# Down projection of a hybrid encoder: six of eleven pairs of K blocks as seven block products

## The chip, the cores and the metric

The kernel runs on one core of one Trainium2 chip. The metric is the device time of one execution in microseconds. TensorE (PE) multiplies, VectorE (DVE), ScalarE (ACT) and GpSimd (POOL) work elementwise, and SyncE (SP) issues most of the DMA transfers. Before the change the median of three runs is 1108.37 us (1108.06 to 1108.92).

## What is computed

Two layers of an encoder on 256 tokens of width 1024, everything in float32: a half-step SwiGLU block, a mixing block with two attention branches, and a second half-step SwiGLU block. The change lies in the SwiGLU blocks, which run four times in all.

```python
D_MODEL = 1024; SEQ = 256; DEPTH = 2; D_FF = 2816

def swiglu(x, w_gate, w_up, w_down):
    return (jax.nn.silu(x @ w_gate) * (x @ w_up)) @ w_down

for l in range(DEPTH):
    x = x + 0.5 * swiglu(rms_norm(x, ffn1_norm[l]), ffn1_w_gate[l], ffn1_w_up[l], ffn1_w_down[l])
    ...
    x = x + merged @ w_out[l]
    x = x + 0.5 * swiglu(rms_norm(x, ffn2_norm[l]), ffn2_w_gate[l], ffn2_w_up[l], ffn2_w_down[l])
```

## The kernel before

**Products.** Tokens stand in two tiles of 128 (t = 0, 1). A float32 number is carried as a high part in the fast matmul format (F32R) and the rest as a low part. `three` (L161) therefore emits three matmuls for each product of a 128x128 block of activations and a 128x512 block of weights: high by high, high by low, low by high.

**Weights.** `load` (L127) fetches 512 KB into one of four raw buffers (`raw`), copies it on ACT into the high part `wh` (L133) and subtracts on DVE to get the low part `wl` (L134). `wh` and `wl` have six buffers each (RING), and one comes back when the last matmul that reads it is done. SP issues the transfers in program order and waits for a free raw buffer at each.

**An FFN.** `ffn` (L294) has a gate/up phase and a down phase. Gate/up runs over eleven chunks c of 256 hidden columns: four loads of two K blocks each, then for each t 24 matmuls (eight K blocks by three) into a bank of `ps_g`, then Silu on ACT (`sg`, L323) and a multiplication on DVE (`hh`, L325). The transposes of `hh` (`turn`, L300) are deferred by H_LAG = 7.9 matmul groups; they write a bank of `ps_tp`, which `split_to` divides into `hi` and `lo` (L176, L177).

The down phase, `out_rows` (L278), runs over 22 rows of K blocks, 128 rows of the weights each. A row's 1024 columns are two halves d of 512. It adds into four PSUM banks acc[t][d], one row at a time (12 matmuls) up to row 17, and the last four rows bank by bank; when a bank is complete, x gets half of it on DVE (L292), and the norm of the next stage is deferred by NORM_LAG = 4 groups. The norm's transposes (L193) read the new x, and what follows them on DVE and ACT (`xg`, `xh`, `xl`) feeds the next stage.

**Order.** PE's order is the order of the program. The orders of DVE, ACT and SP are set by a scheduler when the program is built, each engine then takes its instructions strictly in that order.

Of the kernel before, what the change touches and what calls it, by code (L numbers as in the profile page):

```python
# [48 lines left out]
HEAD = 128  # L49


@with_exitstack
def hybrid_encoder(ctx, tc, x, w_gu1, w_d1, w_in, b_gate, qk_gain, rpb, sink, t5,
# [73 lines left out]
    def load(src, nk, n, tag="raw"):  # L127
        raw = ring.tile([P, 2, 512], F32, name="raw", tag="raw", bufs=RAW)
        wh = ring.tile([P, 2, 512], F32R, name="wh", tag="wh", bufs=RING)
        wl = ring.tile([P, 2, 512], F32R, name="wl", tag="wl", bufs=RING)  # L130
        r, h, lo = (w[:, :nk, :n] for w in (raw, wh, wl))
        nc.sync.dma_start(r, src)
        linked("act", lambda: nc.scalar.activation(h, r, AF.Copy))  # L133
        linked("dve", lambda: nc.vector.tensor_tensor(lo, r, h.bitcast(F32), ALU.subtract))  # L134
        return wh, wl
# [140 lines left out]
    def out_rows(get, nk, w, l, groups, scale, after):  # L276
        acc = [[ps_acc.tile([P, 512], F32, name="acc", tag=tag, bufs=n) for tag, n in pair] for pair in ACC]
        k0 = 0  # L278
        for g in (*[1] * (nk - sum(groups)), *groups):
            pieces = [(k, *rows(w, l, k)) for k in range(k0, k0 + g)]  # L280
            k0 += g
            order = [(d, p) for d in range(2) for p in pieces]
            if k0 < nk:
                order.sort(key=lambda e: e[1][0])
            for t in range(T):
                for d, (k, wh, wl) in order:
                    xh, xl = get(t, k)
                    three(acc[t][d], xh, xl, wh[:, d, :], wl[:, d, :], k == 0, k == nk - 1)
                    tick(1)
                    if k == nk - 1:  # L290
                        xd = xs[t][:, d * 512:(d + 1) * 512]
                        nc.vector.scalar_tensor_tensor(xd, acc[t][d], scale, xd, op0=ALU.mult, op1=ALU.add)  # L292
                        after(t, d)

    def ffn(l, n, w_gu, w_d, after):
        with tc.tile_pool(name="ffn", bufs=1) as fp:
            hs = {}
            tps = {}

            def turn(c, t, hh):  # L300
                if t == 0:
                    tps[c] = ps_tp.tile([P, 2, 2, P], F32, name="tp", tag="tp")
                tp = tps[c]
                for i in range(2):
                    nc.tensor.transpose(tp[:, i, t, :], hh[:, i * P:(i + 1) * P], ident)  # L305
                if t == T - 1:
                    hi = fp.tile([P, 2, 2, P], F32R, name="hi", tag="hi", bufs=NFC)
# [386 lines left out]
```

## Time and profile before

| | us |
|---|---|
| median of three runs | 1108.37 |
| the profiled execution | 1108.37 |
| its span, first to last instruction | 1106.5 |
| first down projection, first matmul to its end | 136.6 to 198.1 |
| DVE waiting for the high part of weights (L134 for L133) | 182.7 in 179 waits |
| ACT waiting for PE in the down projections and w_out (L133 for L164) | 125.2 in 83 waits |

A row of the timeline is: start, duration, engine, line, operation, what it writes and reads, its shape, the count of merged instructions, and in square brackets how long the engine was idle before it and for whom. In a row of groups the duration is the mean of one in nanoseconds. A row of windows gives, for a stretch of the span, the busy time of each engine with its count of instructions, then the granted TensorE clock, the share of the transfers' engines and GB/s. Matmuls overlap in the pipeline, so their distance is read from start to start and not from their duration. A row of transfers gives the median time from issue to landing.

### The profile page before, as it was taken

How to read it: one execution, taken by the hardware profiler on the slowest of the kernel's cores; microseconds unless marked ns; L12 is line 12 of the kernel's file. 1: busy time of each engine (PE TensorE's matmuls, PEld its weight loads, DVE VectorE, ACT ScalarE, POOL GpSimd, SP SyncE). 2: the span in 40 equal slices, each digit the busy share in tenths (PEclk: the TensorE clock that was granted, in tenths of full speed). 3: DMA queues.
4: the chain of work that ended last, by engine and by line, in shares of the span. 5: the costliest groups of instructions: out<-in, count | busy, mean ns of one | idle time of the engine just before them, and what ended most of it. 6: DMA issues, size and time to landing. Idle time of an engine off the chain costs nothing.

```text
span 1106.5 us, 14361 instructions
## 1 busy us (share of the span) xinstructions
PE 1096.3 (99%) x5223; PEld 906.1 (82%) x5223; DVE 700.5 (63%) x987; ACT 600.4 (54%) x914; POOL 103.9 (9%) x101
## 2 busy tenths in 40 slices
PE   9999999999999999999999999999999999999998
PEld 7788888888888888888888888888888888888887
DVE  6655644888887655564475565457888767555542
ACT  6544543788764554454364544347877546454431
POOL 1000000143420000000000000003434000000000
PEclk9999999999999999999999999999999999999999
DMA  7665565765655556556656556647565555646561
GB/s 238 227 188 192 175 212 165 214 189 150 192 183 154 186 175 193 187 176 213 181 156 209 168 187 208 194 119 240 183 190 184 166 171 163 209 161 195 203 192 57
DMA packets 95399, 203.23 MB, mean 184 GB/s; under 512 B 7200, under 2 KB 13376, under 8 KB 95328
## 3 DMA queue, kind: packets, MB, share of 16 engines
q1 hardware_dynamic: 95104, 202.17, 57.7%
q8 instruction: 41, 0.67, 0.3%
q0 software_dynamic: 224, 0.14, 0.1%
q14 instruction: 30, 0.25, 0.1%
HBM read 201.22 MB, written 1.06 MB: 183 GB/s over the span
## 4 chain that ended last, share of the span: by engine, by line
PE 90%; DVE 4%; ACT 3%; issue 2%; DMA 1%; ACTq 0%; DVEq 0%
PE g L162 19%; PE g L164 19%; PE g L163 18%; PE acc L164 9%; PE acc L162 9%; PE acc L163 9%; PE tp L305 2%; DVE wl L134 2%; ACT wh L133 1%; PE tp L193 1%; PE pt L451 1%; PE sc L430 1%; PE g L229 1%; PE po L465 1%; PE br L163 1%
## 5 line engine op out<-in xcount | busy, mean ns | idle before, releaser
L134 DVE TENSOR_TENSOR wl<-raw,wh 128x1024 fp32r<-128x1024 f32 (+1 forms) x368 | 447.0, 1219 | 196.5 <-ACT wh L133 182.7
L133 ACT ACTIVATE wh<-raw 128x1024 fp32r<-128x1024 f32 (+1 forms) x368 | 383.6, 1049 | 209.9 <-PE acc L164 125.2
L162 PE MATMUL g<-wh,xh 128*128 128x512 f32 (+1 forms) x976 | 390.2, 400 | 0.0
L164 PE MATMUL g<-wh,xl 128*128 128x512 f32 (+1 forms) x976 | 379.4, 389 | 0.0
L163 PE MATMUL g<-wl,xh 128*128 128x512 f32 (+1 forms) x976 | 377.8, 387 | 0.4 <-DVE wl L134 0.4
L164 PEld LDWEIGHTS g<-wh,xl 128*128 128x128 f32 x976 | 183.4, 188 | 40.5 <-DVE xl L177 1.3
L163 PEld LDWEIGHTS g<-wl,xh 128*128 128x128 f32 x976 | 184.2, 189 | 31.9 <-DVE wl L134 0.8
L162 PEld LDWEIGHTS g<-wh,xh 128*128 128x128 f32 x976 | 183.7, 188 | 31.5 <-issue 0.9
L323 ACT ACTIVATE sg<-g,rs_y 128x256 f32<-128x256 f32 x88 | 41.7, 474 | 181.6 <-PE g L164 181.4
L162 PE MATMUL acc<-wh,hi 128*128 128x512 f32 x352 | 138.5, 394 | 0.0
L164 PE MATMUL acc<-wh,lo 128*128 128x512 f32 x352 | 137.3, 390 | 0.0
L163 PE MATMUL acc<-wl,hi 128*128 128x512 f32 x352 | 137.1, 389 | 0.0
L325 DVE SCALAR_TENSOR_TENSOR hh<-g,rs_y,sg 128x256 f32<-128x256 f32 x88 | 42.3, 481 | 139.4 <-ACT sg L323 139.4
L164 PEld LDWEIGHTS acc<-wh,lo 128*128 128x128 f32 x352 | 66.1, 188 | 13.9
L163 PEld LDWEIGHTS acc<-wl,hi 128*128 128x128 f32 x352 | 66.2, 188 | 13.4
L162 PEld LDWEIGHTS acc<-wh,hi 128*128 128x128 f32 x352 | 66.1, 188 | 13.3
L168 POOL TENSOR_TENSOR rs_y<-ms,mhalf 128x1 f32<-128x1 f32 x12 | 7.2, 600 | 654.6 <-DVE ms L214 647.4
L443 POOL TENSOR_TENSOR S<-S,sm 128x512 f32<-128x512 f32 x32 | 37.1, 1159 | 71.7 <-DVE sm L442 45.3
L436 ACT ACTIVATE S<-S,mx 128x256 f32<-128x256 f32 x64 | 31.8, 498 | 7.5 <-DVE mx L433 7.4
L305 PEld LDWEIGHTS tp<-ident,hh 128*128 128x128 f32 x176 | 24.6, 140 | 11.3
L292 DVE SCALAR_TENSOR_TENSOR x<-acc,x 128x512 f32<-128x512 f32 x24 | 16.6, 690 | 26.6 <-PE acc L164 26.6
L305 PE MATMUL tp<-ident,hh 128*128 128x128 f32 x176 | 33.3, 271 | 0.0
(133 smaller groups left out, 925.8 us busy)
## 6 DMA issues: line engine op xcount, KB each, us to landing
raw<-in_w_gu SPq DMA_DIRECT2D x176, 512.0 KB, 4.6
raw<-in_w_d SPq DMA_DIRECT2D x88, 512.0 KB, 3.7
raw<-in_w_in SPq DMA_DIRECT2D x64, 512.0 KB, 4.5
raw<-in_w_out SPq DMA_DIRECT2D x16, 512.0 KB, 3.5
bb<-in_b_gate SPq DMA_DIRECT2D x16, 256.0 KB, 3.5
raw<-in_w_bsw SPq DMA_DIRECT2D x8, 512.0 KB, 4.1
raw<-in_w_bna SPq DMA_DIRECT2D x8, 512.0 KB, 3.5
t5b<-vec_d SPq DMA_DIRECT2D x16, 192.0 KB, 3.5
```

The lines of the kernel that those rows point to most:

```text
L133: linked("act", lambda: nc.scalar.activation(h, r, AF.Copy))
L134: linked("dve", lambda: nc.vector.tensor_tensor(lo, r, h.bitcast(F32), ALU.subtract))
L162: nc.tensor.matmul(ps, xh, wh, start=first, stop=False)
L163: nc.tensor.matmul(ps, xh, wl, start=False, stop=False)
L164: nc.tensor.matmul(ps, xl, wh, start=False, stop=last)
L193: nc.tensor.transpose(tp[:, i, :], xs[t][:, k * P:(k + 1) * P], ident)
L292: nc.vector.scalar_tensor_tensor(xd, acc[t][d], scale, xd, op0=ALU.mult, op1=ALU.add)
L305: nc.tensor.transpose(tp[:, i, t, :], hh[:, i * P:(i + 1) * P], ident)
L323: nc.scalar.activation(sg, ps[:, :FC], AF.Silu, scale=rstd[t])
L325: nc.vector.scalar_tensor_tensor(hh, ps[:, FC:], rstd[t], sg, op0=ALU.mult, op1=ALU.mult)
L436: nc.scalar.activation(S_[:, t, :], S_[:, t, :], AF.Exp, bias=mx[:, t:t + 1], scale=-1.0, accum_out=sm[:, t:t + 1])
L443: nc.gpsimd.tensor_tensor(S_, S_, sm.unsqueeze(2).to_broadcast([P, T, S]), ALU.mult)
```

## The change

A pair c is two rows of K blocks (2c and 2c+1), so that the pair's share of the down projection is a product of a 2x2 block matrix of activations (two token tiles by two K blocks) and a 2x2 block matrix of weights (two K blocks by two column halves). For six of the eleven pairs it is now computed as seven block products, in the form with 15 additions known as Strassen's in Winograd's variant. `PLAN` names the kind of each pair: S is the old way, F and G are seven products.

- Activations: for an F or G pair, `turn` copies the four transposed blocks to SBUF on ACT, makes four sums of them on DVE, and splits seven blocks instead of four.
- Weights: `differences` makes four differences of 128x512 blocks on DVE (`u`, `v`), which are then split. For G pairs this is done in the down phase. For F pairs (1 and 3) `prepare` does it beside gate/up, at chunks 2 and 5, into buffers of their own, and the rows are fetched again in the down phase for the blocks used as they are.
- The corner block (product 1) is split into two buffers of 128x512 with tag `xg`, one high and one low.
- Products 2, 3 and 4 add into the banks acc[0][0], acc[0][1], acc[1][0]; products 1, 6, 5, 7 into four extra banks, of `ps_g` and `ps_tp`, over all six pairs.
- After pair 8, `combine` adds the four extra sums into x on DVE (one copy on ACT); pairs 9 and 10 run behind it bank by bank as the last four rows did.
- `out_rows` now takes a range of rows; in S pairs two rows are done bank by bank. Its other user, w_out, is called twice with four rows.

The diff, cut:

```diff
+PLAN = "SFGFGSGSGSS"
+PREP = {2: 1, 5: 3}
+NS = sum(kind != "S" for kind in PLAN)
...
+    def parts(r, nk=2, n=512):
         wh = ring.tile([P, 2, 512], F32R, name="wh", tag="wh", bufs=RING)
         wl = ring.tile([P, 2, 512], F32R, name="wl", tag="wl", bufs=RING)
+        split_to(wh[:, :nk, :n], wl[:, :nk, :n], r)
+        return wh, wl
...
+            SLOT = ((1, 2), (0, 3))
...
             def turn(c, t, hh):
...
-                    split_to(hi, lo, tp)
-                    hs[c] = (hi, lo)
+                m = 4 if PLAN[c] == "S" else 7
+                hi = fp.tile([P, m, P], F32R, name=f"hi{m}", tag=f"hi{m}", bufs=NS if m == 7 else NFC - NS)
+                lo = fp.tile([P, m, P], F32R, name=f"lo{m}", tag=f"lo{m}", bufs=NS if m == 7 else NFC - NS)
+                if m == 7:
+                    a = fp.tile([P, 8, P], F32, name="a", tag="sums", bufs=3)
+                    nc.scalar.activation(a[:, :4, :], tp, AF.Copy)
+                    for to, x, y, op in ((4, 0, 3, ALU.add), (6, 1, 0, ALU.subtract), (5, 4, 1, ALU.subtract),
+                                         (7, 2, 5, ALU.subtract)):
+                        nc.vector.tensor_tensor(a[:, to, :], a[:, x, :], a[:, y, :], op)
+                    split_to(hi, lo, a[:, 1:, :])
+                else:
+                    split_to(hi, lo, tp)
+                hs[c] = (hi, lo)
...
+            def differences(r0, r1, into):
+                sub = lambda to, x, y: nc.vector.tensor_tensor(to, x, y, ALU.subtract)
+                u = fp.tile([P, 2, 512], F32, name="u", tag="sums", bufs=3)
+                sub(u[:, 0, :], r1[:, 1, :], r0[:, 1, :])
+                sub(u[:, 1, :], r0[:, 1, :], r0[:, 0, :])
+                us = into("u", u)
+                v = fp.tile([P, 2, 512], F32, name="v", tag="sums", bufs=3)
+                sub(v[:, 0, :], r1[:, 1, :], u[:, 1, :])
+                sub(v[:, 1, :], r1[:, 0, :], v[:, 0, :])
+                return us, into("v", v)
+
+            def prepare(c):
+                def into(name, r):
+                    hl = [fp.tile([P, 2, 512], F32R, name=f"{name}{p}{c}", tag=f"{name}{p}{c}") for p in "hl"]
+                    split_to(*hl, r)
+                    return hl
+                stored[c] = differences(block_row(2 * c), block_row(2 * c + 1), into)
+
+            def sevens(c):
+                r0 = block_row(2 * c, n=1 if c in stored else 2)
+                r1 = block_row(2 * c + 1)
+                corner = [act.tile([P, 512], F32R, name=f"c{p}", tag="xg", bufs=2) for p in "hl"]
+                split_to(*corner, r0[:, 0, :])
+                low = parts(r1)
+                us, vs = stored.get(c) or differences(r0, r1, lambda name, r: parts(r))
+                half = lambda pair, i: [p[:, i, :] for p in pair]
+                return (("1", 0, corner), ("2", 1, half(low, 0)), ("3", 6, half(low, 1)), ("5", 3, half(us, 1)),
+                        ("6", 4, half(vs, 0)), ("4", 2, half(vs, 1)), ("7", 5, half(us, 0)))
...
+                    for name, slot, (wh, wl) in sevens(c):
...
+                        three(bank, *[h[:, slot, :] for h in hs[c]], wh, wl, first, final and name in extra)
+                        tick(1)
+                    if final:
+                        combine(extra)
...
+                nc.scalar.activation(p1[:, 0, :], acc["1"], AF.Copy, scale=0.5)
...
+                u2 = plus(p1[:, 1, :], "6", p1[:, 0, :])
+                u3 = plus(p16[:, 0, :], "7", u2)
+                u4 = plus(p16[:, 1, :], "5", u2)
+                u5 = plus(ends[:, 0, :], "5", u3)
+                plus(xs[0][:, :512], "1", xs[0][:, :512])
+                for (t, d), u in (((0, 1), u4), ((1, 0), u3), ((1, 1), u5)):
+                    xd = xs[t][:, d * 512:(d + 1) * 512]
+                    nc.vector.tensor_tensor(xd, xd, u, ALU.add)
...
             for c in range(NFC):
...
+                if c in PREP:
+                    prepare(PREP[c])
```

The change moves work on DVE at three places that matter later. Numbers at the ends of names tell the buffers' generations apart.

First place: DVE in the first down projection. Before, it had one split for each row of weights and one low part of activations, here from the seventh row's on (wl_1318):

```order
L134 TENSOR_TENSOR wl_1318<-raw_1316,wh_1317 128x1024
L134 TENSOR_TENSOR wl_1336<-raw_1334,wh_1335 128x1024
L177 TENSOR_TENSOR lo_1241<-tp_1191,hi_1240 128x512
L134 TENSOR_TENSOR wl_1354<-raw_1352,wh_1353 128x1024
L134 TENSOR_TENSOR wl_1372<-raw_1370,wh_1371 128x1024
```

Now, at the same place (wl_1409 is the low part of pair 3's second row, cl_1358 the corner of pair 2, u_1445, v_1452, wl_1442 and wl_1449 belong to pair 4, cl_1405 is the corner of pair 3):

```order
L182 TENSOR_TENSOR wl_1409<-raw_1402,wh_1408 128x1024
L182 TENSOR_TENSOR lo4_1313<-tp_1263,hi4_1312 128x512
L182 TENSOR_TENSOR cl_1358<-raw_1353,ch_1357 128x512
L342 TENSOR_TENSOR u_1445<-raw_1435,raw_1433 128x512
L342 TENSOR_TENSOR v_1452<-raw_1435,u_1445 128x512
L182 TENSOR_TENSOR wl_1442<-raw_1435,wh_1441 128x1024
L342 TENSOR_TENSOR v_1452<-raw_1435,v_1452 128x512
L182 TENSOR_TENSOR wl_1449<-u_1445,wh_1448 128x1024
L182 TENSOR_TENSOR cl_1405<-raw_1400,ch_1404 128x512
```

Work for pair 4 now stands ahead of pair 3's corner, and its first row here waits for the transfer into raw_1435, which by SP's order goes into the buffer that raw_1402 leaves.

Second place: DVE at the end of the first down projection. Before, four updates of x stood there, each behind its bank, and between them the norm of the next stage. Now, from the last row of pair 10 (wl_1679) to the first update (wl_1796 and wl_1802 are weights of the next stage, p1, p16 and ends the combination's sums):

```order
L182 TENSOR_TENSOR wl_1679<-raw_1676,wh_1678 128x1024
L406 SCALAR_TENSOR_TENSOR p1_1646<-g_1342,p1_1646 128x512
L182 TENSOR_TENSOR wl_1796<-raw_1793,wh_1795 128x1024
L406 SCALAR_TENSOR_TENSOR p16_1647<-tp_1349,p1_1646 128x512
L406 SCALAR_TENSOR_TENSOR p16_1647<-tp_1338,p1_1646 128x512
L182 TENSOR_TENSOR wl_1802<-raw_1799,wh_1801 128x1024
L406 SCALAR_TENSOR_TENSOR ends_1648<-tp_1338,p16_1647 128x512
L416 TENSOR_TENSOR x1_83<-x1_83,p16_1647 128x512
L298 SCALAR_TENSOR_TENSOR x0_82<-acc_1282,x0_82 128x512
```

The update x0_82<-acc_1282, which PE's next transposes read, now stands behind eight operations that follow the last weights.

Third place: DVE at chunk 5 of the first FFN's gate/up. Before, the stretch of the same chunks read:

```order
L134 TENSOR_TENSOR wl_660<-raw_658,wh_659 128x1024
L325 SCALAR_TENSOR_TENSOR hh_618<-g_585,rs_y_216,sg_616 128x256
L177 TENSOR_TENSOR lo_613<-tp_554,hi_612 128x512
L134 TENSOR_TENSOR wl_666<-raw_664,wh_665 128x1024
L134 TENSOR_TENSOR wl_672<-raw_670,wh_671 128x1024
L134 TENSOR_TENSOR wl_745<-raw_743,wh_744 128x1024
L325 SCALAR_TENSOR_TENSOR hh_650<-g_620,rs_y_229,sg_648 128x256
```

Now (u_716 and v_723 are differences of pair 3, ul3 and vl3 their stored low parts, a_644 the activations' sums, hh_686 the second hidden tile of chunk 4):

```order
L433 SCALAR_TENSOR_TENSOR hh_654<-g_615,rs_y_216,sg_652 128x256
L342 TENSOR_TENSOR v_723<-raw_714,u_716 128x512
L324 TENSOR_TENSOR a_644<-a_644 128x128 x2
L342 TENSOR_TENSOR v_723<-raw_714,v_723 128x512
L182 TENSOR_TENSOR wl_703<-raw_700,wh_702 128x1024
L324 TENSOR_TENSOR a_644<-a_644 128x128
L182 TENSOR_TENSOR ul3_720<-u_716,uh3_719 128x1024
L182 TENSOR_TENSOR wl_709<-raw_706,wh_708 128x1024
L324 TENSOR_TENSOR a_644<-a_644 128x128
L182 TENSOR_TENSOR vl3_727<-v_723,vh3_726 128x1024
L182 TENSOR_TENSOR wl_806<-raw_803,wh_805 128x1024
L433 SCALAR_TENSOR_TENSOR hh_686<-g_656,rs_y_229,sg_684 128x256
```

Between the two hidden tiles of chunk 4 there are now two differences, their two splits and the activations' sums beside three weight splits, where three weight splits and a low part stood; the first two differences, which wait for raw_714, stand just ahead of hh_654.

98 lines of the change are left out of this document (66 added, 32 removed).

## Prediction

> **What bounds the kernel now.** I read the page first: who is busy, and who stands on the chain of work that ended last.
>
> ```profile
> span 1106.5 us, 14361 instructions
> PE 1096.3 (99%) x5223; PEld 906.1 (82%) x5223; DVE 700.5 (63%) x987; ACT 600.4 (54%) x914; POOL 103.9 (9%) x101
> PEclk9999999999999999999999999999999999999999
> PE 90%; DVE 4%; ACT 3%; issue 2%; DMA 1%; ACTq 0%; DVEq 0%
> ```
>
> TensorE is busy for 99% of the span at a full clock, and holds 90% of the chain. A busy PE need not be PE at its peak, so the next view is the timeline of PE in the first down projection; between the two rows stand 23 more matmuls of the same kind.
>
> ```profile
> 144.41 0.39 PE L162 MATMUL acc<-wh,hi 128*128 128x512 f32 x1
> ...
> 149.85 0.39 PE L162 MATMUL acc<-wh,hi 128*128 128x512 f32 x1
> ```
>
> From the first start to the 25th, 24 matmuls take 5.44 us: one every **0.2267 us**, without a gap. Then the windows: two of 11.4 us, one gate/up chunk each, and one of the down projection.
>
> ```profile
> 90.90:102.30 11.40, 11.40 (x55) 9.37 (x54) 6.48 (x8) 5.58 (x7) 0.00 (x0) 1.00 0.55 185
> 102.30:113.70 11.40, 11.40 (x54) 9.33 (x53) 6.44 (x8) 5.57 (x7) 0.00 (x0) 1.00 0.57 188
> 141.90:191.50 49.60, 49.60 (x222) 41.02 (x221) 22.14 (x20) 19.25 (x20) 0.00 (x0) 1.00 0.62 188
> ```
>
> The columns are PE, PEld, DVE, ACT and POOL. In the down projection DVE works 22.14 of 49.60 us and ACT 19.25; in gate/up DVE works about 6.5 of 11.4. What they idle on says who leads:
>
> ```profile
> 159.98 1.23 DVE L134 TENSOR_TENSOR wl<-raw,wh 128x1024 fp32r<-128x1024 f32 x1 [1.50 <-ACT wh L133]
> 161.61 1.06 ACT L133 ACTIVATE wh<-raw 128x1024 fp32r<-128x1024 f32 x1 [1.66 <-PE acc L164]
> ```
>
> ACT waits for PE to give a weight buffer back, DVE for ACT. Everybody waits for PE, so a matmul taken away is time taken away, as long as DVE and ACT keep ahead.
>
> At this place the Trainium skill, "Perfetto Trace Analysis", section "Identifying the Most-Contended Engine", speaks against me: it calls matmul occupancy a bad measure and asks for the share of weight loads, which is 82% here. If each removed pair were worth only its load, 188 ns by the page's costliest groups, the gain below would be 13.5 us and not 16.3. The trace disagrees so far: 41.02 of 49.60 is 83%, and 0.188 / 0.2267 is 83% too, so 83% is what an unbroken row of these matmuls looks like.
>
> **The change part by part.** *Removed.* A pair of K blocks took 2 rows x 2 halves x 2 token tiles x 3 = 24 matmuls; seven products x 3 are 21. Six pairs, four FFNs: 72 matmuls less (all of 128x512), 72 x 0.2267 = **16.3 us**. The transposes stay.
>
> *Added on DVE and ACT.* Durations come from the groups by shape, and the distance from start to start on a DVE that has all its inputs from the timeline:
>
> ```profile
> L134 DVE TENSOR_TENSOR wl<-raw,wh 128x1024 fp32r<-128x1024 f32 x360 | 441.8, 1231 | 195.3 <-ACT wh L133 181.6
> L133 ACT ACTIVATE wh<-raw 128x1024 fp32r<-128x1024 f32 x360 | 379.0, 1058 | 208.4 <-PE acc L164 125.2 <-PE g L164 68.3 <-PE br L164 8.7
> L325 DVE SCALAR_TENSOR_TENSOR hh<-g,rs_y,sg 128x256 f32<-128x256 f32 x88 | 42.3, 481 | 139.4 <-ACT sg L323 139.4
> L177 DVE TENSOR_TENSOR xl<-xg,xh 128x512 fp32r<-128x512 f32 x24 | 16.5, 688 | 6.4 <-ACT xh L176 6.3
> L176 ACT ACTIVATE xh<-xg 128x512 fp32r<-128x512 f32 x24 | 15.0, 625 | 18.6 <-DVE xg L200 18.6
> ...
> 196.99 1.23 DVE L134 TENSOR_TENSOR wl<-raw,wh 128x1024 fp32r<-128x1024 f32 x1 [0.69 <-ACT wh L133]
> 198.13 0.69 DVE L177 TENSOR_TENSOR xl<-xg,xh 128x512 fp32r<-128x512 f32 x1
> 198.73 0.68 DVE L292 SCALAR_TENSOR_TENSOR x<-acc,x 128x512 f32<-128x512 f32 x1
> ```
>
> So in a row a 128x1024 op costs 1.14 us of DVE and a 128x512 op 0.60. A pair with kind G needs four subtractions (2.4), three 128x1024 splits (3.42) and a corner split (0.60): 6.4 us of DVE against 21 x 0.2267 = 4.76 us of PE. DVE loses 1.7 us on such a pair. A pair S needs 2 x 1.14 = 2.3 against 5.44, a pair F 1.14 + 0.60 = 1.7 against 4.76: they win 3 us each. Over pairs 1 to 8 (two F, four G, two S) DVE needs 33.7 us and PE 39.4. On average it fits; what counts is the order. I follow it by hand, with 0 at pair 1's first product, so that pairs 2, 3, 4 start on PE at 4.76, 9.52, 14.28.
>
> *Pair 3's corner.* DVE takes pair 4's differences ahead of cl_1405, pair 3's corner, which PE's second matmul of pair 3 wants at 9.75. Pair 4's second row can be fetched only into the buffer that wl_1409 frees. That split's weight buffer comes back six matmuls and two transposes before 0, at about -1.4; ACT 1.06 and DVE 1.23 later it is 0.95.
>
> ```profile
> raw<-in_w_gu SPq DMA_DIRECT2D x176, 512.0 KB, 4.6
> raw<-in_w_d SPq DMA_DIRECT2D x88, 512.0 KB, 3.7
> ...
> x<-in_x SPq DMA_DIRECT2D x3, 256.0 KB, 6.1
> ```
>
> Landing after 3.7 gives 4.65; then u, v, wl_1442, v, wl_1449, cl_1405 are 0.60 + 0.60 + 1.14 + 0.60 + 1.14 + 0.69 = 4.77, so 9.42: 0.33 us to spare. With gate/up's 4.6 it is 10.3, a stall of 0.6; it can't fall below nothing, since PE has no gap to gain. I take **0.2** per FFN, nearer to the 3.7 row. Behind it each hand-worked arrival has 2.5 us or more in hand up to pair 8 (pair 6's last split ends at 21.5 and is wanted at 27).
>
> *The combination.* After pair 8 stand eight more DVE operations, among them the two pieces of the next stage's weights. The old place, in the timeline of DVE and PE:
>
> ```profile
> 188.81 0.69 DVE L292 SCALAR_TENSOR_TENSOR x<-acc,x 128x512 f32<-128x512 f32 x1 [0.40 <-PE acc L164]
> 191.34 0.60 PE L193 MATMUL tp<-ident,x 128*128 128x128 f32 x4
> ```
>
> The update ended at 189.50, 1.84 us before PE's transposes read it. Now, with 0 at pair 9's first matmul, the transposes come 24 matmuls on, at 5.44. wl_1679's buffer is freed by pair 8's third product at -2.5; ACT copies product 1 first and splits by -1.5, DVE ends at -0.25. Then p1 0.60, wl_1796 (waits 0.25 for ACT) 1.14, p16 0.69 and 0.60, wl_1802 (ready at 2.0, no wait) 1.14, ends 0.60, x1 0.60 and x0<-acc 0.69 sum to 6.3 and end at 6.06: PE waits 0.6. Bounds: with whole durations in place of the pitch (+0.09 on eight) 1.35; if only what follows product 7 counted, 0.2 + 0.69 + 0.60 + 1.14 + 3 x 0.60 + 0.09 = 4.5, nothing. I take **0.65** for three FFNs. The last has neither next weights nor transposes: nothing.
>
> *Work prepared beside gate/up.* Two chunks get 4 x 0.60 + 2 x 1.14 = 4.7 us of DVE each, and six chunks per FFN get sums of the activations: four 128x128 ops and a split of 896 columns in place of 512 (+0.4). No row has a 128x128 DVE op of this kind; between nothing and the 481 ns of hh the four cost 0 to 1.9 us, taken near 1. A chunk has 11.4 - 6.5 = 4.9 us free, so only the prepared ones overrun, by 1 to 2 us, into a neighbour that is free. What could be late is hh of the chunk before, behind the stored splits: wanted 5.44 us into the chunk. Counting from raw_714's landing (-4.9 with 3.9 us) the rows up to hh_686 sum to 9.5: 4.6, so 0.8 to spare; with a landing of 4.6 and whole durations it is 0.9 late. Bounds 0 to 0.9, taken at **0.1** for eight chunks.
>
> The Trainium skill, "VectorE: DVE Perf Modes", section "The TRN2 errata", gives an fp32 tensor_tensor of N columns as (N+151)/0.96 ns, an estimate of 0.29 us for 128 columns. With that the four cost 1.2 and the sum doesn't change; for 512 columns it gives 0.69, which the 688 ns row bears out.
>
> *At no cost.* ACT's extra splits and copies (in the down projection a G pair needs 3 x 1.06 + 0.63 = 3.8 of 4.76 us; without that room they would delay the same DVE chain). The prepared rows are fetched twice, less one half: 8 x 0.79 = 6.3 MB on top of 203, which the transfers' idle share hides:
>
> ```profile
> DMA packets 95399, 203.23 MB, mean 184 GB/s; under 512 B 7200, under 2 KB 13376, under 8 KB 95328
> q1 hardware_dynamic: 95104, 202.17, 57.7%
> ```
>
> *Sum.* -16.3 + 3 x 0.65 + 4 x 0.2 + 8 x 0.1 = -12.7 us. The profiled execution took 1108.37 us, which is also the median of the runs, 1.9 us of it outside the span; so **1095.7 us**, a span of 1093.8.
>
> **The rivals.** (1) *Nothing is late*: all covers hold, 1108.4 - 16.3 = 1092.1. For it: 0.33 and 0.8 us in hand at two places; against it: the combination has none. (2) *DVE becomes the bound.* With whole durations in place of the pitch, DVE ends 0.1 late at pair 3, 1.35 at the combination and 0.2 in each prepared chunk: 4 x 1.85 less the last 1.35 gives back 6.0, so 1098.1. With gate/up's landing of 4.6 on top, all upper bounds at once, pair 3 is 1.0 late and each prepared chunk 0.9: 4 x 4.15 - 1.35 = 15.3 back, 1107.4. The middle is 1102.7. For it: DVE has 5.7 us of slack over eight pairs and takes its waits in strict order. Against: the pitch of 0.60 and 1.14 in the busiest part of the trace. (3) *The raw buffers become the bound, and it is slower.* Four buffers, now held until the corner's split, put a whole landing into each step of SP's queue. Beyond 4.0 us a landing delays pair 3 by the excess, and beyond 4.7 both prepared chunks: (L - 4.0) + 0.65 + 2 (L - 4.7) eats the 4.07 us per FFN at L = 5.6. At 6.1, the first row of x, it gives back 22 us: 1114. Against: 3.7 and 4.6 are medians under the same load. (4) *Weight loads set the pace*: 13.5 in place of 16.3, 1098.5, the case that the first-named page's rule would make; the even 0.2267 speaks against it. That the matmuls aren't removed is excluded: PE's order has 4769 rows before and 4697 after.
>
> **How the numbers follow.** Forecast (1093.5 to 1098) 0.62; nothing late 0.11; DVE the bound 0.18; weight loads 0.03; raw buffers 0.06, of which 0.04 end slower. The range takes in the forecast with its bounds, rival 1 and the lower half of rival 2: 1092 to 1103. Faster by over 0.2% (about what a measurement of this kernel tells from no change, 2.2 us): 0.92; within: 0.04; slower: 0.04.
>
> **What would show it.** Right: 72 fewer matmuls at the old pitch; PE gaps of 0.3 to 1 us only at the transposes of x behind three of the down projections; small ones at pair 3. Wrong: a pitch that isn't 0.2267 within the seven products; gaps released by wl, u or v at pairs 4 to 8 (rival 2); SP's wait for buffers followed by ACT waiting for raw (rival 3).

## The result, and the profile after

| | before | after |
|---|---|---|
| median of the runs, us | 1108.64 (4 runs, 1108.06 to 1109.42) | 1098.09 (4 runs, 1095.75 to 1098.78) |
| the profiled execution, us | 1108.37 | 1095.75 |
| its span, us | 1106.5 | 1093.9 |

The ratio is 0.9901, with a 95% interval of 0.9883 to 0.9918: 10.5 us less, where 12.7 were forecast. The profiled execution is the lowest of the four, and it equals the forecast (1095.7). The other three stand 1.7 to 3.0 us above it, while the kernel before has a spread of 1.4 us. The median lies 2.4 us above the forecast, and meets the 1098.1 of the prediction's second rival (DVE as the bound). So there are two questions: whether the terms of the sum were right in the execution that came out as forecast, and what the others have on top. Of the others, only a later one, of 1099.06 us, was profiled (`again`, below).

The page of the changed kernel, with the rows of the list of waits that are new or have changed most:

```profile
span 1093.9 us, 14598 instructions
PE 1081.7 (99%) x5151; PEld 891.3 (81%) x5151; DVE 834.9 (76%) x1259; ACT 651.1 (60%) x990; POOL 106.2 (10%) x101
PE 82%; DVE 9%; ACT 3%; DMA 3%; issue 3%; ACTq 0%; DVEq 0%
raw<-in_w_d SPq DMA_DIRECT2D x96, 512.0 KB, 4.5
...
DVE u L342 <- DMA raw<-in_w_d: 68.4, 40, 3.9
DVE wl L182 <- ACT wh L181: 65.6, 88, 4.4
ACT wh L181 <- DMA raw<-in_w_d: 42.7, 18, 5.6
```

There are 72 matmuls less. DVE has 134 us more to do, and its wait for the high parts of weights has gone from 182.7 to 65.6 us: a split on DVE now waits less often for ACT's copy. DVE's new wait, 68.4 us, is for transfers, and the median transfer of a row of the down projection now lands after 4.5 us in place of 3.7. ACT waits for rows of the down projection too, 42.7 us, which it did nowhere before; the prediction had named such a wait as a sign that the raw buffers set the pace. PE holds 82% of the chain in place of 90%; DVE and the transfers have taken the difference.

Two of the places at which the forecast put what is given back. First pair 4's differences and pair 3's corner (cl), with the matmul that waits for it, in the timelines of DVE and PE:

```profile
147.52 0.69 DVE L342 TENSOR_TENSOR u<-raw 128x512 f32<-128x512 f32 x1 [2.37 <-DMA raw<-in_w_d]
148.13 0.68 DVE L342 TENSOR_TENSOR v<-raw,u 128x512 f32<-128x512 f32 x1
148.74 1.22 DVE L182 TENSOR_TENSOR wl<-raw,wh 128x1024 fp32r<-128x1024 f32 x1
149.87 0.68 DVE L342 TENSOR_TENSOR v<-raw,v 128x512 f32<-128x512 f32 x1
150.47 1.22 DVE L182 TENSOR_TENSOR wl<-u,wh 128x1024 fp32r<-128x1024 f32 x1
151.61 0.68 DVE L182 TENSOR_TENSOR cl<-raw,ch 128x512 fp32r<-128x512 f32 x1
...
151.89 0.39 PE L167 MATMUL g<-ch,hi 128*128 128x512 f32 x1
152.35 0.50 PE L168 MATMUL g<-cl,hi 128*128 128x512 f32 x1
152.68 0.40 PE L169 MATMUL g<-ch,lo 128*128 128x512 f32 x1
...
188.20 0.66 PE L198 MATMUL tp<-ident,x 128*128 128x128 f32 x4 [0.42 <-DVE x L298]
```

From the start of u to the end of cl are 4.77 us, as added up by hand. What differs is the arrival. These are the steps ahead of it, on ACT, PE, DVE and SP:

```profile
141.64 1.06 ACT L181 ACTIVATE wh<-raw 128x1024 fp32r<-128x1024 f32 x1 [3.53 <-PE acc L169]
142.26 0.48 PE L167 MATMUL g<-ch,hi 128*128 128x512 f32 x1
142.73 1.23 DVE L182 TENSOR_TENSOR wl<-raw,wh 128x1024 fp32r<-128x1024 f32 x1 [0.24 <-ACT wh L181]
143.98 0.33 SPq L338 DMA_DIRECT2D raw<-in_w_d  x1
```

Pair 1's first product started at 142.26, so u began at 5.26 on the forecast's clock and not at 4.65. The matmul on cl starts 0.46 us after the one ahead of it in place of 0.23, and the one behind it after 0.33, so this wait cost 0.34 us. The last row of the first of these two views is the transposes of x behind the first down projection; they wait for the update of x.

### The profile page after: what moved, and what is told of

The parts are those of the page before. It is cut to its first block, busy times and chain, and to the rows that moved or that the text cites. A ratio compares the mean times of both kernels' runs of the same rounds, so it can differ in the third digit from the quotient of the medians.

```text
span 1093.9 us, 14598 instructions
## 1 busy us (share of the span) xinstructions
PE 1081.7 (99%) x5151; PEld 891.3 (81%) x5151; DVE 834.9 (76%) x1259; ACT 651.1 (60%) x990; POOL 106.2 (10%) x101
## 4 chain that ended last, share of the span: by engine, by line
PE 82%; DVE 9%; ACT 3%; DMA 3%; issue 3%; ACTq 0%; DVEq 0%
PE g L167 18%; PE g L169 18%; PE g L168 18%; PE acc L167 5%; PE acc L169 5%; PE acc L168 5%; DVE wl L182 4%; DMA raw<-in_w_d 2%; ACT wh L181 2%; PE tp L313 2%; PE tp L198 1%; PE pt L555 1%; PE sc L534 1%; PE g L234 1%; PE po L569 1%
## 5 line engine op out<-in xcount | busy, mean ns | idle before, releaser
L182 DVE TENSOR_TENSOR wl<-raw,wh 128x1024 fp32r<-128x1024 f32 (+1 forms) x344 | 412.9, 1214 | 69.0 <-ACT wh L181 65.6
L181 ACT ACTIVATE wh<-raw 128x1024 fp32r<-128x1024 f32 (+1 forms) x344 | 354.1, 1045 | 165.8 <-PE g L169 47.6
L167 PE MATMUL acc<-wh,hi 128*128 128x512 f32 x224 | 88.3, 394 | 0.0
L169 PE MATMUL acc<-wh,lo 128*128 128x512 f32 x224 | 87.3, 390 | 0.0
L168 PE MATMUL acc<-wl,hi 128*128 128x512 f32 x224 | 87.3, 390 | 0.0
L342 DVE TENSOR_TENSOR u<-raw 128x512 f32<-128x512 f32 x48 | 33.2, 691 | 68.8 <-DMA raw<-in_w_d 68.4
L169 PEld LDWEIGHTS acc<-wh,lo 128*128 128x128 f32 x224 | 42.0, 188 | 8.9
L168 PEld LDWEIGHTS acc<-wl,hi 128*128 128x128 f32 x224 | 42.1, 188 | 8.7 <-DVE wl L182 0.2
L167 PEld LDWEIGHTS acc<-wh,hi 128*128 128x128 f32 x224 | 42.1, 188 | 8.5
```

The costliest lines, as they stand in the source:

```text
L167: nc.tensor.matmul(ps, xh, wh, start=first, stop=False)
L168: nc.tensor.matmul(ps, xh, wl, start=False, stop=False)
L169: nc.tensor.matmul(ps, xl, wh, start=False, stop=last)
L181: linked("act", lambda: nc.scalar.activation(hi, src, AF.Copy))
L182: linked("dve", lambda: nc.vector.tensor_tensor(lo, src, hi.bitcast(F32), ALU.subtract))
L342: sub = lambda to, x, y: nc.vector.tensor_tensor(to, x, y, ALU.subtract)
```

## The experiments

The theory (A in the expectations): the matmuls are worth their pitch, and what is given back is made on DVE, which takes its instructions in strict order; work that PE needs soon stands there behind work that waits for a transfer. The rivals are that DVE has too much work in whatever order, that a matmul was worth less than its pitch, and that a wait only moves when its place is mended.

### The changed kernel again, and its two halves

`again` is the changed kernel without an edit.

> The changed kernel once more, for its spread: four runs so far lie between 1095.75 and 1098.78 us, against 1108.06 to 1109.42 before the change. Theory A (what is given back is DVE's chain of differences and corners, which waits for the landing of raw rows, plus the combination): another profile shows PE's gaps at the same places, pair 3's corner, the transposes of x behind a down projection and those of hh at a prepared chunk, and a longer span goes with longer gaps there: 3 us more span, 3 us more in gaps at wl, u and cl. Rival B (the spread lies in a stage that the change doesn't touch): the gaps at these places stay as in the first profile, some 4 us in all, whatever the span.

1097.42 us (1096.48 to 1099.06), ratio 0.9900 (0.9887 to 0.9914). Its profile fell into the execution of 1099.06, so the two profiles of one program show what 3.3 us are made of; they are compared below. Of the 3.4 us by which the spans differ (1097.3 against 1093.9), about 2 lie at the expected places and 1.4 at a place in the mixing block that the expectation did not name, so each side was right in part.

`removed_only` is the kernel before, less as many matmuls as the change removes:

```diff
-                    three(acc[t][d], xh, xl, wh[:, d, :], wl[:, d, :], k == 0, k == nk - 1)
+                    if not (nk > KD and (t, d) == (1, 1) and k in (3, 5, 7, 9, 13, 17)):
+                        three(acc[t][d], xh, xl, wh[:, d, :], wl[:, d, :], k == 0, k == nk - 1)
```

> The kernel before with 18 matmuls of each down projection left out (token tile 1, right half, K rows 3, 5, 7, 9, 13 and 17: that share of the sum is missing), and nothing added: the price of 72 matmuls by itself. Theory A: 72 x 0.2267 = 16.3 us less than before, 1092.3. Rival C (a removed matmul is worth only its weight load, 0.188): 13.5 less, 1095.1. The spread should be that of the kernel before, some 1 us.

1091.88 us (1091.79 to 1093.79), ratio 0.9850 (0.9837 to 0.9864): 16.7 us for 72 matmuls (15.1 to 18.1 by the interval), where the pitch of 0.2267 gives 16.3. The case in which the weight loads set the pace, 13.5 us, is out, and with it the prediction's reading of the Trainium skill, "Perfetto Trace Analysis", section "Identifying the Most-Contended Engine", that the 82% of the loads say more than the 99% of the matmuls: here each matmul taken away was worth 0.232 us, not the 0.188 us of its load. This also serves as a floor: about what a version of the change with these 5151 matmuls can reach if nothing that it adds is late.

`no_differences` is the changed kernel with the rows of weights themselves split in place of their differences:

```diff
-                u = fp.tile([P, 2, 512], F32, name="u", tag="sums", bufs=3)
-                sub(u[:, 0, :], r1[:, 1, :], r0[:, 1, :])
...
-                return us, into("v", v)
+                us = into("u", r0)
+                return us, into("v", r1)
```

> The changed kernel without the 16 subtractions of weight blocks of 128x512 on DVE that the four G pairs of each FFN take, and without those of the two F pairs: rows r0 and r1 are split as they come, so the seven products use wrong blocks. All matmuls, splits, transfers and the combination stay. Theory A: pair 3's corner comes in time, the combination's gap stays: 1.2 to 1.5 us less than the changed kernel on the same chip in its best runs, and the spread shrinks to about 1 us. Rival B: no difference in time or spread beyond 0.5 us.

1094.18 us (1093.59 to 1094.97), ratio 0.9870 (0.9857 to 0.9884): 3.2 us less than `again`, over twice what was expected, with less spread. In its profile the gaps at cl, at the transposes of hh and at those of qs (below) are absent. Everything else of the change is still there, and so is one of its waits, at the transposes of x behind three of the down projections:

```profile
187.88 0.66 PE L198 MATMUL tp<-ident,x 128*128 128x128 f32 x4 [0.43 <-DVE x L298]
```

It starts 0.82 us behind the matmul ahead of it all three times, 0.58 more than without a wait. So 3 x 0.58 = 1.7 us belong to the combination alone, and about 3 us go away with the differences, though DVE's four subtractions of 0.60 us for each of six pairs are 58 us of work: nearly all of it is hidden.

### Less room on DVE

Two kernels change which pairs are prepared beside gate/up. `none_prepared` makes all six pairs' differences in the down phase, `prepared_pairs_together` puts the prepared pairs one behind the other:

```diff
-PLAN = "SFGFGSGSGSS"
-PREP = {2: 1, 5: 3}
+PLAN = "SGGGGSGSGSS"
+PREP = {}
```

```diff
-PLAN = "SFGFGSGSGSS"
-PREP = {2: 1, 5: 3}
+PLAN = "SFFGGSGSGSS"
+PREP = {2: 1, 5: 2}
```

> All six pairs of kind G, at the same places of the plan (S G G G G S G S G S S), nothing prepared beside gate/up: the same 72 matmuls less. By the pitch of 1.14 and 0.60 DVE needs 6 x 6.42 + 2 x 2.28 = 43.1 us over pairs 1 to 8, PE 39.4. Theory A (DVE's room in the down phase is the limit): the four G pairs in a row fall behind by 4 x 1.7 = 6.6 us less a lead of 2 to 3, and PE waits at wl, u or cl for 2 to 6 us per FFN: 1102 to 1116. Rival E (only the landings and the combination matter): within 1.5 us of the changed kernel.

> The plan S F F G G S G S G S S: the second prepared pair is pair 2 in place of pair 3, so that both prepared pairs come first. Same work. Theory A: DVE gets 6 us ahead over two F pairs, pair 3 (now G) has its rows earlier, the corner gaps go: 0.5 to 1.5 us less than the changed kernel. Rival: two G pairs in a row (12.8 us of DVE against 9.5 of PE) with four raw buffers wait for landings at pair 4, and it is equal or up to 2 us slower.

1102.07 us (1101.29 to 1104.49) and 1102.17 us (1101.14 to 1104.60), both at a ratio of 0.9947 (0.9935 to 0.9960): 4.7 us more than `again`, at the lower edge of what was expected of the first, and the wrong way for the second. I had expected a gain there, since pair 3's corner then has no differences ahead of it. The timeline of PE in the first of the two shows the new wait:

```profile
174.40 0.50 PE L168 MATMUL acc<-wl,hi 128*128 128x512 f32 x1 [0.42 <-DVE wl L182]
```

and in the second:

```profile
709.31 0.50 PE L168 MATMUL acc<-wl,hi 128*128 128x512 f32 x1 [1.17 <-DVE wl L182]
```

PE waits here for a plain split behind a run of G pairs. In `none_prepared` DVE is late with work: in the 5 us ahead of the split it is not idle, and by the prediction's numbers it loses 1.7 us on each G pair, with four in a row. In `prepared_pairs_together` that is not what the trace shows at the wait above. There DVE had stood idle for a transfer, shortly before the split:

```profile
706.82 0.69 DVE L342 TENSOR_TENSOR u<-raw 128x512 f32<-128x512 f32 x1 [3.67 <-DMA raw<-in_w_d]
```

Nor had the corner's gap gone. It stood one pair earlier, at pair 2's corner, where pair 3's differences are now ahead: 0.2, 0.8 and 0.7 us in three of the four FFNs. So this run speaks rather for the rival of its expectation, the wait for landings with four raw buffers, though it cost more than the rival's 2 us. DVE's total is the same in this kernel as in the changed one, so it is the order of the pairs that costs 4.7 us; how much of it is DVE's backlog and how much the transfers, no run separates.

### The order at each place

`update_first` issues the first update of x ahead of five of the combination's operations, three of which stood ahead of it:

```diff
-                u4 = plus(p16[:, 1, :], "5", u2)
-                u5 = plus(ends[:, 0, :], "5", u3)
...
+                def rest():
+                    u4 = plus(p16[:, 1, :], "5", u2)
+                    u5 = plus(ends[:, 0, :], "5", u3)
...
+            def after_bank(t, d):
+                if remaining:
+                    with tc.issue_after(updated[0].ins):
+                        remaining.pop()()
+                after(t, d)
```

`weights_held` leaves the combination as it is, and puts the low parts of the next stage's weights behind that update (and behind the same update after w_out, which uses the same helper):

```diff
+        with ExitStack() as order:
+            if behind is not None:
+                order.enter_context(tc.issue_after(behind.ins))
+            return linked("dve", lambda: nc.vector.tensor_tensor(lo, src, hi.bitcast(F32), ALU.subtract))
...
+                    if (t, d) == (0, 0):
+                        updated[0] = done
```

`corner_first` leaves both as they are, and puts pair 4's differences behind pair 3's corner (pair 4 is the only one to which the condition applies):

```diff
-                us, vs = stored.get(c) or differences(r0, r1, lambda name, r: parts(r))
+                with ExitStack() as order:
+                    if PLAN[c - 1:c + 1] == "FG" and c > 2:
+                        order.enter_context(tc.issue_after(last_corner[0].ins))
+                    us, vs = stored.get(c) or differences(r0, r1, lambda name, r: parts(r))
+                last_corner[0] = own
```

> The changed kernel with DVE's order turned at one place: the first update of x (from acc[0][0]) goes ahead of the combination's sums with product 5 and of the four additions that need them. Same work. Theory A: the first profile's gaps before the transposes of x (0.81, 1.10 and 0.81 us, against 0.2 to 0.3 without a wait) close, 1.5 to 2.1 us less than the changed kernel. If instead the whole chain is late there, the second half's transposes take over the wait, and less than 0.5 us is gained.

> The changed kernel with one rule of order added: DVE's low parts of the next stage's weights go behind the first update of x. Same work. In the second profile of the changed kernel DVE idled 0.69 us ahead of the second of these pieces, for a transfer that landed late, with the update queued behind it. Theory A: without the two pieces the update ends some 4.1 us into pair 9, ahead of the transposes at 5.44, whatever lands when: the three gaps before the transposes of x close, 2 to 3 us less than the changed kernel. Rival D (DVE is late by its sum there, and any order moves the wait): the second half's transposes or the next stage's take it over, and less than 0.7 us is gained.

> The changed kernel with pair 4's differences behind pair 3's corner on DVE. Same work. Theory A: the gaps at pair 3's corner close (0.23, 0.15, 0.36 and 0.19 us over the kernel without differences in the first profile, up to 0.9 in the second) and pair 4 keeps its 2.5 us in hand: 0.9 to 1.7 us less than the changed kernel. Rival D: the gaps come back at pairs 4 to 8, and nothing is gained.

`update_first` gave 1098.93 us (1096.17 to 1099.48), ratio 0.9907 (0.9894 to 0.9921), and `weights_held` 1097.61 us (1096.80 to 1098.22), ratio 0.9900 (0.9885 to 0.9915): no gain in either, both expectations missed. In `update_first` the wait moved to the second half of the same transposes, since the operations put behind the first update stand ahead of the second. There it was 0.7, 0.1 and 0.3 us, so the three places together were better than in the changed kernel, but other gaps of this profile hid it, 1.5 us at qs (below) and 1.0 at the transposes of hh:

```profile
192.53 0.66 PE L198 MATMUL tp<-ident,x 128*128 128x128 f32 x4 [0.57 <-DVE x L300]
```

In `weights_held` all three waits at these transposes were gone, as meant, but others were larger in its profile, at pair 3's corner and at the transposes of qs in the mixing block (below):

```profile
695.44 0.50 PE L170 MATMUL g<-cl,hi 128*128 128x512 f32 x1 [1.60 <-DVE cl L187]
```

`corner_first` gave 1094.76 us (1093.97 to 1095.11), ratio 0.9875 (0.9862 to 0.9889), 2.7 us less than `again`, on another chip, and more than expected. It was repeated on a third chip as `corner_first_again`, beside `both_orders`, which is `corner_first` and `weights_held` together (here too pair 4's differences alone are moved, not pair 6's):

> The corner order alone, unchanged from corner_first, beside both_orders on one chip: 1094 to 1095.5 if the gain of 2.7 us over the changed kernel was the order's and not the chip's or the hour's; 1096 or more if it was.

> Both reorderings at once: pair 4's and 6's differences behind the corner of the pair before, and the low parts of the next stage's weights behind the first update of x. Nothing is left out of the computation. Theory A (each of the two is a queue on DVE of its own, and the second one's gain of 3 x 0.6 to 0.8 us was hidden in weights_held by the backlog that the corner order takes away): 1.5 to 2.5 us less than the corner order alone, 1092.2 to 1093.3. Rival (the split of the next stage's weights is needed anyway, so the wait moves to the first products of the next stage, at the transposes of qs or at g<-wh,xl): within 0.7 us of the corner order, 1094 to 1095.5, with new gaps there.

1096.34 us (1095.17 to 1097.37), ratio 0.9887 (0.9873 to 0.9902), for the repetition, and 1094.63 us (1094.31 to 1096.71), ratio 0.9877 (0.9861 to 0.9894), for both. By the test that its expectation set, 1096 or more, the repetition does not confirm 2.7 us: the corner order is worth 1.1 to 2.7 us over `again` by the times. The profiles say more. In both the gap at cl is gone at all four places; what the repetition has on top stands elsewhere, 3.2 us at the transposes of x and 1.4 at those of qs, against 2.3 and none in the first. Both orders together are 1.7 us below the corner order on the same chip, as the theory had it, but the intervals overlap, 1094.63 lies in the rival's range, and the profile half agrees with the rival: the three gaps at the transposes of x are gone, and a gap of 1.71 us (0.23 of it the pitch) stands at the transposes of qs.

### GpSimd, and the last two places

That gap comes and goes. Of the twelve profiles so far six show it once. It goes back to GpSimd: the low part of qs waits, through qn, for `rs_y`, a power of eight numbers a row on GpSimd. The timeline of `again`, where the gap was:

```profile
753.47 2.36 DVE L182 TENSOR_TENSOR wl<-raw,wh 128x1024 fp32r<-128x1024 f32 x2
757.37 0.76 DVE L465 TENSOR_TENSOR qn<-z,rs_y 128x512 f32<-128x512 f32 x1 [1.54 <-POOL rs_y L173]
...
746.04 1.65 POOL L173 TENSOR_TENSOR rs_y<-hv,mhalf 128x8 f32<-128x8 f32 x1 [1.99 <-DVE hv L463]
753.71 3.62 POOL L173 TENSOR_TENSOR rs_y<-hv,mhalf 128x8 f32<-128x8 f32 x1 [1.25 <-DVE hv L463]
...
761.59 0.84 PE L478 MATMUL tp<-ident_r,qs 128*128 128x128 f32 x8 [1.20 <-DVE hv L463]
```

and of the first profile of the changed kernel, where it was not:

```profile
751.99 2.37 DVE L182 TENSOR_TENSOR wl<-raw,wh 128x1024 fp32r<-128x1024 f32 x2
754.75 0.83 DVE L465 TENSOR_TENSOR qn<-z,rs_y 128x512 f32<-128x512 f32 x1 [0.39 <-POOL rs_y L173]
...
752.19 2.53 POOL L173 TENSOR_TENSOR rs_y<-hv,mhalf 128x8 f32<-128x8 f32 x1 [1.03 <-DVE hv L463]
```

Here the operation takes 2.53 or 3.62 us, and both times it starts 0.2 us into the first of two splits of DVE. Where it starts ahead of a split, as at 746.04, it takes 1.65, even if by only 0.05 us as in the kernel before. When it starts second, it ends 1.5 us after the end of the first split (751.99 + 1.22) in the one case, and 1.5 us after the end of both (753.47 + 2.36) in the other, and the gap stands in exactly the six profiles with 3.62.

`queries_first` adds to `both_orders` that the low part of qs stands ahead of the next two splits on DVE, and `all_orders` adds to that the fourth place, beside gate/up: the low part of v of a prepared pair stands behind hh of the chunk before.

```diff
             for token in ORDER.split():
+                if token == "k0":
+                    updated[0] = low["Q1"]
...
+                low[key] = split_to(qs[:, :, 0, :], qs[:, :, 1, :], qn)
```

```diff
-                    split_to(*hl, r)
+                    split_to(*hl, r, last_hh[0] if name == "v" else None)
```

> both_orders with one more edit: in the mixing block, the low part of the second tile's queries (qs) stands ahead of two splits of weights on DVE, which are wanted later. Nothing is left out of the computation. What is tested is the gap of 1.4 to 1.75 us at PE's transposes of qs, which six profiles show once and six don't. Theory A: it is made on GpSimd: rs_y<-hv,mhalf takes 3.62 us in place of 1.65 to 2.5 in exactly the profiles that have the gap, because two splits of DVE run behind each other while it runs, and qs has no time in hand behind it; with qs two splits (2.3 us) earlier the gap is gone even where rs_y takes 3.62 us, and the median is 0.7 to 1.5 us below both_orders, ratio 0.9860 to 0.9870. Rival (the gap is the time which the last reordering moved, and it moves on): the gap shows up behind it, at kn or at the first products with the two splits, and the ratio stays at 0.9877.

> queries_first with the fourth place in order too: beside gate/up the low part of v of a prepared pair stands behind hh of the chunk before, which PE's transposes of hh wait for. Nothing is left out of the computation. Theory A: the gaps of 0.2 to 1.0 us at these transposes are DVE's queue as well, so 0.5 to 1.5 us less than queries_first, ratio 0.985 to 0.986, near the 1091.9 us that the 72 matmuls alone would leave. Rival (DVE's total of work in the prepared chunk is what is late, in whatever order): no gain, and the wait comes at a later split of weights of that chunk.

`queries_first`: 1094.08 us (1092.57 to 1094.49), ratio 0.9866 (0.9850 to 0.9883), in the range that was expected, though the gain of 0.55 us falls short of 0.7 and the interval takes in 0.9877. Its profile decides more than its time: rs_y took 3.62 us again, and PE's gap fell from 1.71 to 0.35 us, as the timeline of GpSimd and PE shows:

```profile
211.34 3.62 POOL L175 TENSOR_TENSOR rs_y<-hv,mhalf 128x8 f32<-128x8 f32 x1 [1.23 <-DVE hv L475]
...
217.29 0.39 PE L171 MATMUL g<-wh,xl 128*128 128x512 f32 x1
217.64 0.84 PE L492 MATMUL tp<-ident_r,qs 128*128 128x128 f32 x8
```

`all_orders`: **1092.42 us** (1092.02 to 1093.06), ratio 0.9854 (0.9840 to 0.9869). It is below both kernels, 5.0 us below `again` (the intervals of the ratios, 0.9840 to 0.9869 and 0.9887 to 0.9914, do not meet), and cannot be told from the floor of `removed_only`, 0.9850. The gap of 1.2 us that `queries_first` still had at the transposes of hh (at 934.92) is gone. Its page:

```profile
span 1090.2 us, 14594 instructions
PE 1080.1 (99%) x5151; PEld 892.3 (82%) x5151; DVE 833.1 (76%) x1259; ACT 649.5 (60%) x990; POOL 108.2 (10%) x101
PE 92%; DVE 4%; ACT 3%; issue 2%; DMA 0%; ACTq 0%; DVEq 0%
raw<-in_w_d SPq DMA_DIRECT2D x96, 512.0 KB, 4.3
```

DVE and ACT do what they did, and the median row still lands after 4.3 us, but PE has 92% of the chain. The same corner and the same junction in its timelines of DVE and PE:

```profile
148.63 1.22 DVE L187 TENSOR_TENSOR wl<-raw,wh 128x1024 fp32r<-128x1024 f32 x1 [3.44 <-ACT wh L183]
149.77 0.68 DVE L187 TENSOR_TENSOR cl<-raw,ch 128x512 fp32r<-128x512 f32 x1
150.37 1.29 DVE L351 TENSOR_TENSOR u<-raw 128x512 f32<-128x512 f32 x2
...
185.90 0.68 DVE L303 SCALAR_TENSOR_TENSOR x<-acc,x 128x512 f32<-128x512 f32 x1
186.50 1.22 DVE L187 TENSOR_TENSOR wl<-raw,wh 128x1024 fp32r<-128x1024 f32 x1
...
151.92 0.39 PE L169 MATMUL g<-ch,hi 128*128 128x512 f32 x1
152.15 0.39 PE L170 MATMUL g<-cl,hi 128*128 128x512 f32 x1
...
187.29 0.60 PE L203 MATMUL tp<-ident,x 128*128 128x128 f32 x4
```

The corner is done at 150.45, 1.7 us before PE takes it, and u, v and their splits follow when they can. The update of x ends at 186.58, and no matmul waits there.

## Why the prediction was right, and where it was not

The sizes come from PE's timelines: the start of every matmul in the two profiles of the changed kernel, against the start of the same matmul in the profile of `all_orders`, summed by place. At the corner the matmul behind the one that waited starts a further 0.11 us late; that is counted in.

| us given back at | forecast | execution of 1095.75 | execution of 1099.06 |
|---|---|---|---|
| pair 3's corner, four times | 0.8 | 1.4 | 1.7 |
| the combination, three times | 1.95 | 2.0 | 3.4 |
| transposes of hh | 0.8 | 0.3 | 0.6 |
| transposes of qs | none | 0 | 1.4 |
| sum | 3.55 | 3.7 | 7.1 |

The sums are the whole differences of the spans (1093.9 and 1097.3 us against 1090.2). That 3.7 comes so near to 3.55 is in part luck: the corner took 0.6 more than forecast and the transposes of hh 0.5 less. The median's nearness to the 1098.1 of the second rival is not its mechanism, since whole durations in place of the pitch are not what the rows of DVE show.

- **The matmuls removed**: 16.3 us forecast, 16.7 measured alone. Shown.
- **Pair 3's corner**: the row of six DVE operations was right to the hundredth. The landing was right too: although the median row landed after 4.5 us, this one did after 3.5 (issued at 143.98, with u starting at 147.52), and after 3.3 to 3.5 in the other three down projections, where 3.7 was forecast. The term that was mis-sized is the one ahead of it, "about -1.4": the weight buffer came free with the fourth matmul before pair 1's first product (start at -1.05) and not with the sixth, ACT could begin at -0.62, and the split of pair 3's second row ended at 1.70 and not at 0.95. In two of the four it ended later still, since another of pair 4's differences, which needs its first row alone, stood ahead of this split on DVE; the list of the first place begins just behind it, and the prediction left it out. In `again` that row landed late once, and this made the largest gap at cl, 0.92 us over the pitch:

```profile
1042.68 0.69 DVE L342 TENSOR_TENSOR u<-raw 128x512 f32<-128x512 f32 x1 [2.71 <-DMA raw<-in_w_d]
```

  So the corner cost 0.34 us on average and not 0.2. That the corner's place on DVE is the cause is shown by `corner_first` and its repetition: with these differences behind it the gap at cl is gone from both profiles.
- **The combination**: 0.65 each was right in the execution of 1095.75 (0.58, 0.86 and 0.58 us), and too little in general. This is the step that failed: "wl_1802 (ready at 2.0, no wait)". In the first profile ACT was done with its high part at 2.02 after pair 9's first matmul, in `again` at 3.70, because its weights landed late, and the whole of DVE stood behind it. At the other two places of `again` it was the first piece, wl_1796, that could start only at 1.30 and 0.81, where 0.6 was forecast. (Between the split of the last weights, wl_1679, and the update stand seven operations, not the eight told of at the second place; the prediction's sum takes them as they are.) The timelines of ACT and DVE in `again`:

```profile
184.78 1.06 ACT L181 ACTIVATE wh<-raw 128x1024 fp32r<-128x1024 f32 x1 [2.06 <-DMA raw<-in_w_in]
...
185.88 1.23 DVE L182 TENSOR_TENSOR wl<-raw,wh 128x1024 fp32r<-128x1024 f32 x1 [0.69 <-ACT wh L181]
187.02 0.68 DVE L406 SCALAR_TENSOR_TENSOR ends<-tp,p 128x512 f32<-128x512 f32 x1
187.62 0.68 DVE L416 TENSOR_TENSOR x<-x,p 128x512 f32<-128x512 f32 x1
188.22 0.69 DVE L298 SCALAR_TENSOR_TENSOR x<-acc,x 128x512 f32<-128x512 f32 x1
```

  and in the first profile:

```profile
183.13 1.06 ACT L181 ACTIVATE wh<-raw 128x1024 fp32r<-128x1024 f32 x1 [0.38 <-DMA raw<-in_w_in]
...
187.46 0.68 DVE L298 SCALAR_TENSOR_TENSOR x<-acc,x 128x512 f32<-128x512 f32 x1
```

  The update does not need these weights; it only stands behind them. I priced the late landing at pair 3 and beside gate/up, in the second rival, and not here. `weights_held` shows the cause: with the weights behind the update the gap is gone three times out of three.
- **Work prepared beside gate/up**: 0.8 forecast, 0.3 and 0.6 measured, at one and at two of eight chunks. Later profiles had up to 1.2 at one chunk, beyond the bound of 0.9. The four sums of the activations, taken near 1 us, are 1.00 in the trace. `all_orders`, with vl behind hh, has no gap there.
- **At no cost**: GpSimd was not among the engines I looked at, and its 3.62 us cost 1.4 us in one of the two profiles of the changed kernel. What the change has to do with it is that DVE's row of splits now comes at another time; that the change alone makes it come is not shown, since the kernel before, where this operation took 1.64 us both times, has one profile, and there it started ahead of the splits by 0.05 us only.
- **The rivals**: "nothing late" (1092.1) was not the changed kernel, but it is `all_orders` (1092.42), so the forecast's split into matmuls and waits holds. "DVE becomes the bound" in the sense of too much work is out for this order of pairs, since `all_orders` does the same work; `none_prepared` shows that it is near. "Weight loads" is out by `removed_only`. "The raw buffers" did not come as a bound: the median landing went to 4.5 us, not beyond 5.6, though 11 of the 104 landings of the down projections' rows took more than 5.6 in the first profile, the longest 6.9. ACT's wait for raw rows, its sign, did come, and in `all_orders` 21.0 us of it stand without PE waiting.

What stays open: why one mended place brought no gain in `weights_held` while it brought 1.7 us on top of the corner order. Its profile had larger gaps at the corner, 0.3 to 1.8 us over the pitch, and one of 1.3 at qs. The largest goes back, through the buffers, to a transfer of that down projection's rows that took 6.2 us, where the one issued at the same point took 3.8 to 4.8 in the two profiles of the changed kernel; whether the later weights had a part in it was not tried.

## What to carry to other kernels

When work is added to an engine that has room on average, list for each moment what PE needs next and what stands ahead of it in that engine's queue; a wait for a transfer there is a wait for all behind it, needed or not. Put what is wanted soonest ahead of what may be late, at every such place at once, since here one mended alone often left the time where it was. A sum over one profiled execution holds for landings as they were in that execution, so give each term that follows a transfer a second price, with the landing at the slow end of the trace.

## What the runs showed of the hardware

- Two executions of one program differ by which transfer lands late. The second of the next stage's transfers was issued at 179.32 us in the first profile and at 179.30 in `again`, and ACT could begin on it at 183.13 and at 184.78: 3.8 and 5.5 us for the same 512 KB. With less in the queue behind such a transfer less of it was seen: the spread of the runs is 3.3 us for the changed kernel over eight executions, and 1.0 for `all_orders` over four.
- A short operation on GpSimd takes up to more than twice its time when it starts within splits on DVE (1.65, 2.53 and 3.62 us). The Trainium skill, "SBUF — State Buffer", section "🔬 SBUF: two separate sides", says that GpSimd and a DVE operation with two SBUF inputs take the same port pair as an exclusive lock, and the one that comes second waits. The ends, 1.5 us behind one split or behind both, agree with that. The other way round the trace does not: splits on DVE that started within the operation, 0.05 us into it in the kernel before and 0.4 us into the row at 746.04 of `again`, took their usual 1.23 and 0.69 us. Why the operation gets in between the two splits at one time and not at another, no run here shows, and no run took the splits away.
